# Four conditioning matmuls held together, and up-projection blocks of 384 columns with a copied halo

## The chip, the cores and the metric

The kernel runs on one core of one Trainium2 chip. The metric is device microseconds of one execution, and a kernel's time is the median of several runs. TensorE (PE) does the matmuls, VectorE (DVE) and ScalarE (ACT) read the results out of PSUM, GpSimd (POOL) works on SBUF alone, and SyncE (SP) issues the DMAs.

## The reference

A two-layer trunk runs one step for a prompt of 1024 positions and for 8 samples of 16 positions. The kernel treats the 1024 + 128 = 1152 rows together. Width is 1024, the MLP is 2816 wide, everything is fp32. What matters here is the conditioning and the channel mixer:

```
ada = sc @ w_ada[l] + b_ada[l]                  # sc = silu(c); one row for the prompt, eight for the samples
h = x * (1 + sc_f) + sh_f
u = h @ w_up                                    # 1024 -> 2 * 2816
y = conv_b
for tap in range(3):                            # causal depthwise convolution over positions
    y = y + conv_w[tap] * ue[:, tap : tap + T]  # ue = u with two rows of state in front
a, g = split(y)
out = (gelu(g) * a) @ w_down
x = layer_norm(ALPHA * x + (1 + gate) * out)
```

Position t of the convolution needs u at t, t-1 and t-2. So a block of positions needs the last two columns of the block ahead of it; these are called the halo here.

## The kernel before

The order of the work is: conditioning group 0; the first projection input; attention of layer 0 (sliding window); its output projection; the MLP of layer 0; attention of layer 1 (which begins with the key and value projections); its output projection; the MLP of layer 1.

**Split operands.** A product in nearly full fp32 is made from three products of rounded operands: each operand is split into a rounded high part and the rest (`split`, L147 to L151: ACT or DVE rounds, L149/L151; DVE or POOL subtracts, L160). `wload` brings one weight block of 512 KB into the ring `ws` of two slots and splits it into `wh` and `wl`. `mmT` (L265) multiplies one weight block with all of `H`: eight matmuls with `wl`, then sixteen with `wh`, 24 in all, into one PSUM bank, with positions as columns.

**Blocks of positions.** `BLK` cuts the 1152 positions in three blocks of 384. The key, query and other transposed projections use `BLK`. The up-projection uses its own cut, so that a block holds its halo by computing it again:

```
UB = ((0, 384), (380, 388), (764, 388))
```

**The MLP** (`ffn`). `up(j, gg)` loads one weight block of 128 up-projected channels, and calls `up_block` for the three blocks. There are 22 values of j and two halves gg (0 is `a`, 1 is the gated half), so 44 groups of channels in each layer. The three blocks take the PSUM banks 0, 1 and 2 in turn (`ub`). `conv` reads the bank: ACT takes the third tap and the bias (L980), DVE adds the other taps (L983; four shorter ones in the last block, which holds 256 prompt positions and the samples), and in the gated half ACT applies gelu (L1027), POOL multiplies (L1029), and ACT and DVE split the product for the down-projection (L149, L160). `down` (L1054, `dmm`) multiplies two groups into the row sums `acc` through the banks 3 to 5. The last pair of groups is done by `down_last`, in which the blocks of both halves alternate: block 0 of half 0, block 0 of half 1, block 1 of half 0, and so on, through the same three banks.

**Conditioning** (`ada`). Each of 7 groups of 2048 columns is made in 8 steps k. A step loads two weight blocks of 512 KB (L207), and issues four matmuls (L209), each with 32 stationary columns in its own quarter of the array (`tile_position=(0, 32 * j)`) and its own quarter of PSUM's partitions. Each of the four is two instructions in the trace, so a step is eight. Matmuls j = 0, 1 read the first block and j = 2, 3 the second. Group 0 runs at the start. Groups 1 and 2 are spread as background steps over attention 0, where their blocks use the two `ws` slots that the weights of the query projection use too; groups 3 to 6 are spread over the MLP of layer 0, with a ring of three slots of their own.

**Order.** The framework places every engine's instructions by a simulated timeline: at each point it takes from the ready ones the earliest in program order. It adds all semaphores, and it orders any two accesses of one PSUM bank. `issue_after(x)` holds an instruction back until x has been placed. Engines run their own queue in order, SP's DMA issues among them.

Of the kernel before, what the change touches and what calls it, by code (L numbers as in the profile page):

```python
# [20 lines left out]
BLK = ((0, 384), (384, 384), (768, 384))  # L21
# [66 lines left out]
class Trunk:  # L88
# [100 lines left out]
    def ada(self, gi, bank, ring=None, row=None):  # L189
        nc = self.nc  # L190
        ring = ring or self.ws
        ps = self.bank(bank)

        def load_bias(row):
            bsrc = self.I["adab"][gi : gi + 1, :]
            for j in range(4):
                nc.sync.dma_start(
                    row[32 * j : 32 * j + 32, 512:1024],
                    bass.AP(bsrc.tensor, bsrc.offset + j * 512, [[0, 32], [1, 512]]),
                )  # L200

        if row is not None:
            load_bias(row)
        for k in range(8):
            w = [ring.next() for _ in range(2)]
            for hf in range(2):
                nc.sync.dma_start(w[hf], self.I["adaw"][gi, k, hf])  # L207
            for j in range(4):
                nc.tensor.matmul(  # L209
                    ps[32 * j : 32 * j + 32, :],  # L210
                    self.cT[:, k * 32 : k * 32 + 32],
                    w[j // 2][:, (j % 2) * 512 : (j % 2) * 512 + 512],
                    start=k == 0,
                    stop=k == 7,
                    tile_position=(0, 32 * j),
                )
            yield
        if row is None:
            row = ring.next()
            load_bias(row)  # L220
        nc.vector.tensor_add(row[:, 0:512], ps, row[:, 512:1024])
        yield
        gate = {1: (0, 0), 2: (1, 2), 5: (2, 0), 6: (3, 2)}.get(gi)
        if gate is not None:
            g, j0 = gate
            for j2 in range(2):
                r = slice(32 * (j0 + j2), 32 * (j0 + j2) + 32)
                nc.gpsimd.tensor_scalar_add(row[r, 512:1024], row[r, 0:512], 1.0)
                nc.sync.dma_start(
                    self.gd[g, :, j2 * 512 : j2 * 512 + 512],  # L230
                    row[32 * (j0 + j2) : 32 * (j0 + j2) + 9, 512:1024],
                )
        for i in range(4):
            nc.tensor.transpose(ps[:, i * 128 : i * 128 + 128], row[:, i * 128 : i * 128 + 128], self.ident)
        dst = self.adaT[:, gi * 144 : gi * 144 + 144].rearrange("p (j i r) -> p i j r", j=4, i=4)
        nc.vector.tensor_copy(dst, ps.rearrange("p (i j r) -> p i j r", i=4, j=4)[:, :, :, 0:9])
        yield
# [710 lines left out]
    def ffn(self, l, xsrc, xdst, affs):  # L948
        nc, I, O, H = self.nc, self.I, self.O, self.H
# [26 lines left out]

        def conv(ps, cc, bi, y):
            w = lambda i: cw[:, cc, i : i + 1]
            off = 0 if bi == 0 else 4
            nc.scalar.activation(y, ps[:, off : off + 384], AF.Identity, bias=w(3), scale=w(2))  # L980

            def tap(o, u, i):
                nc.vector.scalar_tensor_tensor(o, u, w(i), o, op0=ALU.mult, op1=ALU.add)  # L983

            if bi == 0:
                tap(y[:, 1:384], ps[:, 0:383], 1)
                tap(y[:, 2:384], ps[:, 0:382], 0)
            elif bi == 1:
                tap(y, ps[:, 3:387], 1)
                tap(y, ps[:, 2:386], 0)  # L990
            else:
                tap(y[:, 0:256], ps[:, 3:259], 1)
                tap(y[:, 0:256], ps[:, 2:258], 0)
                ys = y[:, 256:384].rearrange("p (s q) -> p s q", q=16)
                us = ps[:, 260:388].rearrange("p (s q) -> p s q", q=16)
                tap(ys[:, :, 1:16], us[:, :, 0:15], 1)
                tap(ys[:, :, 2:16], us[:, :, 0:14], 0)
                nc.gpsimd.tensor_add(ys[:, :, 0:2], ys[:, :, 0:2], E4[:, cc])

        UB = ((0, 384), (380, 388), (764, 388))  # L1000

        acts = {}
        ya = {}
# [1 line left out]
        def up(j, gg):  # L1005
            w = self.wload(I["wup"][l, j + 22 * gg])
            for bi in range(3):
                up_block(w, j, gg, bi)

        def up_block(w, j, gg, bi):  # L1010
            cc = j + 22 * gg
            s0, n = UB[bi]
            ps = self.bank(ub.next())
            self.mmT(w, ps, s0, n)
            if gg == 0:
                y = ya[bi] = self.ya.next()
            else:
                y = self.yg.next()
            conv(ps, cc, bi, y)
            if bi == 2:  # L1020
                uo = self.uo[gg].rearrange("p (j s r) -> p j s r", s=9, r=2)
                src = ps[:, 258:402].rearrange("p (s q) -> p s q", q=16)[:, :, 0:2]
                nc.scalar.copy(uo[:, j % 11], src)
                if j % 11 == 10:
                    nc.sync.dma_start(O["conv"][l, gg, j // 11], self.uo[gg])
            if gg == 1:
                nc.scalar.activation(y, y, AF.Gelu_apprx_tanh)  # L1027
                a = self.at.next()
                nc.gpsimd.tensor_mul(a, y, ya[bi])  # L1029
                h, lo = aring.next()  # L1030
                self.split(a, h, lo, "a", "v")
                acts[(j, bi)] = (h, lo)
# [25 lines left out]
        def down_last():  # L1058
# [12 lines left out]
            for t in LO[l]:  # L1071
                for bi in UP[l].get(t, ()):
                    for gg in range(2):
                        up_block(wu[gg], NFF - 1, gg, bi)
                    if bi == 2:
                        w = [self.wring.next() for _ in range(2)]
                        for s, x in zip(wr, w):
                            self.split(s, *x, "a", "v")
# [267 lines left out]
```

## Time and profile before

| | |
|---|---|
| three runs | 3056.77, 3062.35 and 3062.54 us, median 3062.35 |
| profiled execution | 3055.63 us, of which the span of the instructions is 3053.6 us |
| PE busy | 2857.6 us, 94% of the span |
| DVE, ACT, POOL busy | 50%, 37%, 27% |
| mean granted TensorE clock | 0.968 |

The stages by the trace: conditioning group 0 and the first input up to about 100 us, attention 0 to 380, its output projection to 560, the MLP of layer 0 to about 1480, the key and value projections to 1650, attention 1 to 2020, its output projection to 2200, and the MLP of layer 1 to the end. In the timeline rows a line stands for a run of like instructions: start, length, engine, line, shape and count. The length goes to the modelled end of the last one, so the distance between matmuls is read from one row's start to the next row's start.

### The profile page before, as it was taken

Reading aid. Unit: us, or ns where it says so; the run is one execution under the profiler, and the core shown is the slowest. Engines: PE = TensorE matmul, PEld = TensorE weight load, DVE = VectorE, ACT = ScalarE, POOL = GpSimd, SP = SyncE. Lnnn points to the kernel's source line nnn. Section 1 sums busy time; section 2 is a strip of 40 time slices with the busy share of each in tenths; the row PEclk is TensorE's granted clock in tenths of the full one; section 3 lists DMA queues with packets and bytes.
Section 4 is the critical chain, followed back from the end, with each engine's and each line's share of the span. In section 5 each row is a group of like instructions: output and inputs, shape, how many; then the busy total and the mean of one; then the engine's idle time right before and its main releaser. Section 6 shows DMA issues by size and latency. Waiting matters only on the chain.

```text
span 3053.6 us, 42727 instructions
## 1 busy us (share of the span) xinstructions
PE 2857.6 (94%) x16524; PEld 2556.2 (84%) x16524; DVE 1516.3 (50%) x3162; ACT 1129.9 (37%) x2400; POOL 834.8 (27%) x599
## 2 busy tenths in 40 slices
PE   7999868899999999998999999966999999999996
PEld 4987656789888898997999988754899999999995
DVE  4355657524443443358412667655824444444468
ACT  2465613432222222224435766631432222222224
POOL 2011113422222222354651100102522222222253
PEclk8999888999999999999999999988999999999998
DMA  8555484622222222223785467778311111111121
GB/s 296 171 169 182 135 167 124 230 101 76 90 80 81 85 77 97 80 70 113 272 281 182 127 171 211 200 170 170 126 50 42 42 42 43 43 42 42 42 89 73
DMA packets 228235, 372.79 MB, mean 122 GB/s; under 512 B 35368, under 2 KB 149864, under 8 KB 227648
## 3 DMA queue, kind: packets, MB, share of 16 engines
q1 hardware_dynamic: 228032, 370.06, 39.6%
q8 instruction: 130, 2.13, 0.3%
q14 instruction: 73, 0.60, 0.1%
HBM read 294.65 MB, written 84.79 MB: 124 GB/s over the span
## 4 chain that ended last, share of the span: by engine, by line
PE 75%; DMA 9%; DVE 8%; SPq 3%; issue 2%; POOL 2%; ACT 2%; DVEq 0%; ACTq 0%; POOLq 0%
PE PS L265 45%; PE PS L1054 15%; PE PS L277 3%; PE PS L549 3%; PE PS L530 2%; PE PS L209 2%; PE PS L504 1%; DMA F<-rD 1%; SPq L923 1%; PE PS L507 1%; PE PS L651 1%; DMA x1att<-rD 1%; SPq L928 1%; POOL wl L160 1%; DVE F L944 1%
## 5 line engine op out<-in xcount | busy, mean ns | idle before, releaser
L265 PE MATMUL PS<-H,wh 128*128 128x384 f32 (+1 forms) x5472 | 1048.5, 339 | 0.3 <-DVE H L160 0.3
L265 PEld LDWEIGHTS PS<-H,wh 128*128 128x128 f32 x5472 | 968.1, 189 | 18.0 <-issue 9.2
L983 DVE SCALAR_TENSOR_TENSOR F<-PS,F 128x256 f32<-128x256 f32 (+2 forms) x704 | 353.1, 512 | 540.2 <-ACT F L980 527.1
L160 POOL TENSOR_TENSOR wl<-ws,wh 128x1024 fp32r<-128x1024 f32 x167 | 406.2, 2438 | 769.8 <-ACT wh L149 737.0
L265 PE MATMUL PS<-H,wl 128*128 128x384 f32 (+1 forms) x2736 | 570.2, 345 | 18.0 <-DVE H L151 7.9
L265 PEld LDWEIGHTS PS<-H,wl 128*128 128x128 f32 x2736 | 491.3, 191 | 49.7 <-issue 15.1
L1054 PE MATMUL PS<-wh,X 128*128 128x512 f32 x1584 | 465.5, 393 | 12.0 <-DVE acc L1045 4.2
L980 ACT ACTIVATE F<-PS,F 128x384 f32<-128x384 f32 x264 | 177.3, 672 | 744.4 <-PE PS L265 738.9
L1054 PEld LDWEIGHTS PS<-wh,X 128*128 128x128 f32 x1584 | 294.2, 188 | 73.1 <-issue 6.7
L1045 DVE TENSOR_TENSOR acc<-acc,PS 128x512 f32<-128x512 f32 x324 | 221.4, 686 | 268.8 <-PE PS L1054 268.2
L1029 POOL TENSOR_TENSOR F<-F 128x384 f32<-128x384 f32 x132 | 137.8, 1044 | 656.3 <-ACT F L1027 653.8
L1054 PE MATMUL PS<-wl,X 128*128 128x512 f32 x792 | 246.6, 392 | 0.0
L149 ACT CAST wh<-ws 128x1024 fp32r<-128x1024 f32 x176 | 182.2, 1045 | 139.0 <-PE PS L1054 75.1
L277 PE MATMUL PS<-wh,H 128*128 128x256 f32 (+1 forms) x1008 | 197.1, 325 | 36.9 <-DVE H L160 36.2
L277 PEld LDWEIGHTS PS<-wh,H 128*128 128x128 f32 x1008 | 153.3, 197 | 52.0 <-DVE H L160 37.4
L1054 PEld LDWEIGHTS PS<-wl,X 128*128 128x128 f32 x792 | 149.3, 188 | 33.2
L160 DVE TENSOR_TENSOR X<-F,X 128x384 fp32r<-128x384 f32 x132 | 111.2, 842 | 102.2 <-ACT X L149 101.9
L160 POOL TENSOR_TENSOR H<-F,H 128x1024 fp32r<-128x1024 f32 x23 | 60.3, 2622 | 257.6 <-ACT H L149 172.3
L470 DVE CUSTOM_DVE_ANT_0 F<-PS,F,C 128x256 f32<-128x256 f32 (+3 forms) x208 | 96.9, 480 | 60.8 <-PE PS L507 36.5
L530 PE MATMUL PS<-C,F 128*128 128x128 f32 x720 | 119.7, 281 | 5.5 <-DVE X L536 2.8
L1027 ACT ACTIVATE F<-F 128x384 f32<-128x384 f32 x132 | 69.1, 524 | 140.6 <-DVE F L983 128.2
L277 PE MATMUL PS<-x1att,H 128*128 128x512 f32 x432 | 114.5, 413 | 0.0
(196 smaller groups left out, 3119.3 us busy)
## 6 DMA issues: line engine op xcount, KB each, us to landing
ws<-in_wup_dram SPq DMA_DIRECT2D x88, 512.0 KB
F<-in_adaw_dram SPq DMA_DIRECT2D x74, 512.0 KB
ws<-in_wdn_dram SPq DMA_DIRECT2D x44, 512.0 KB
ws<-in_adaw_dram SPq DMA_DIRECT2D x32, 512.0 KB
X<-oT SPq DMA_DIRECT2D x64, 256.0 KB
x1att<-kH SPq DMA_DIRECT2D x60, 256.0 KB
xd<-F SPq DMA_DIRECT2D x27, 512.0 KB
F<-xd SPq DMA_DIRECT2D x27, 512.0 KB
```

The source lines that it names most:

```text
L149: nc.scalar.copy(out, in_)
L160: self.eng(el).tensor_sub(lo, src, hi.bitcast(F32))
L265: self.nc.tensor.matmul(out[:, 0:n], w[a][:, k * 128 : k * 128 + 128], H[:, p, k, s0 : s0 + n], start=i == 0, stop=i == 23)
L277: self.nc.tensor.matmul(out[:, 0:n], H[:, p, j * kn + k, t0 : t0 + 128], w[a][:, k * n : k * n + n], start=i == 0, stop=i == 23,)
L470: nc.vector.tensor_tensor_reduce(out=p[:, c0 : c0 + w], in0=ps, in1=b, scale=1.0, scalar=init, op0=ALU.add, op1=ALU.min, accum_out=nm)
L530: nc.tensor.transpose(t[:, m * 128 : m * 128 + 128], p[:, (kt - k0) * 128 : (kt - k0) * 128 + 128], self.ident)
L549: nc.tensor.matmul(ob[:, i0 * 128 : i0 * 128 + w], vst[a][:, kt, :], pp[:, m1 : m1 + w], start=cnt == 0, stop=cnt == 2 * len(order) - 1, s ...
L980: nc.scalar.activation(y, ps[:, off : off + 384], AF.Identity, bias=w(3), scale=w(2))
L983: nc.vector.scalar_tensor_tensor(o, u, w(i), o, op0=ALU.mult, op1=ALU.add)
L1029: nc.gpsimd.tensor_mul(a, y, ya[bi])
L1045: nc.vector.tensor_add(row[:, n], row[:, n], ps)
L1054: nc.tensor.matmul(ps, ac[m][p][:, cs], w[m][q][:, n], start=i == 0, stop=i == 5)
```

## The change

Two things change. In `ada` the four matmuls of a step are issued in the order j = 2, 3, 0, 1, and the last three are held behind the first, which reads the block that is loaded second. In `ffn` the up-projection uses the three blocks of 384 without overlap. In blocks 1 and 2 the matmuls write from column 2 of the bank, and ACT then copies the last two columns of the block before, from that block's PSUM bank, into columns 0 and 1. The columns that `conv` reads move by two.

```diff
-            for j in range(4):
-                nc.tensor.matmul(
...
+            lead = None
+            for j in (2, 3, 0, 1):
+                with ExitStack() as es:
+                    if lead is not None:
+                        es.enter_context(self.tc.issue_after(lead))
+                    mm = nc.tensor.matmul(
...
+                if lead is None:
+                    lead = mm.ins
...
-            off = 0 if bi == 0 else 4
+            off = 0 if bi == 0 else 2
...
-                tap(y, ps[:, 3:387], 1)
-                tap(y, ps[:, 2:386], 0)
+                tap(y, ps[:, 1:385], 1)
+                tap(y, ps[:, 0:384], 0)
...
-        UB = ((0, 384), (380, 388), (764, 388))
+        halo = {}
...
-            s0, n = UB[bi]
+            s0, n = BLK[bi]
             ps = self.bank(ub.next())
-            self.mmT(w, ps, s0, n)
+            off = 0 if bi == 0 else 2
+            self.mmT(w, ps[:, off:512], s0, n)
+            if bi:
+                nc.scalar.copy(ps[:, 0:2], halo.pop(cc))
+            if bi < 2:
+                halo[cc] = ps[:, off + 382 : off + 384]
...
-                src = ps[:, 258:402].rearrange("p (s q) -> p s q", q=16)[:, :, 0:2]
+                src = ps[:, 256:400].rearrange("p (s q) -> p s q", q=16)[:, :, 0:2]
```

More of the change, by code (lines that the diff above doesn't have):

```diff
@@ L207, in ada @@
                 nc.sync.dma_start(w[hf], self.I["adaw"][gi, k, hf])
-            for j in range(4):
[L209 to L216, printed above, removed]
+            lead = None
[4 more added lines that the diff above has]
+                    mm = nc.tensor.matmul(
+                        ps[32 * j : 32 * j + 32, :],
+                        self.cT[:, k * 32 : k * 32 + 32],
+                        w[j // 2][:, (j % 2) * 512 : (j % 2) * 512 + 512],
+                        start=k == 0,
+                        stop=k == 7,
+                        tile_position=(0, 32 * j),
+                    )
+                if lead is None:
+                    lead = mm.ins
             yield
@@ L988, in conv @@
             elif bi == 1:
-                tap(y, ps[:, 3:387], 1)
-                tap(y, ps[:, 2:386], 0)
-            else:
-                tap(y[:, 0:256], ps[:, 3:259], 1)
-                tap(y[:, 0:256], ps[:, 2:258], 0)
+                tap(y, ps[:, 1:385], 1)
+                tap(y, ps[:, 0:384], 0)
+            else:
+                tap(y[:, 0:256], ps[:, 1:257], 1)
+                tap(y[:, 0:256], ps[:, 0:256], 0)
                 ys = y[:, 256:384].rearrange("p (s q) -> p s q", q=16)
-                us = ps[:, 260:388].rearrange("p (s q) -> p s q", q=16)
+                us = ps[:, 258:386].rearrange("p (s q) -> p s q", q=16)
                 tap(ys[:, :, 1:16], us[:, :, 0:15], 1)
```

## The prediction

> **What bounds the kernel now.** I read the page first, for the engine on which the end hangs, and then the busy time by stage, since the change touches stages that may have different limits. The page's busy times and its chain of waits by line:
>
> ```profile
> span 3053.6 us, 42727 instructions
> PE 2857.6 (94%) x16524; PEld 2556.2 (84%) x16524; DVE 1516.3 (50%) x3162; ACT 1129.9 (37%) x2400; POOL 834.8 (27%) x599
> ...
> PE PS L265 45%; PE PS L1054 15%; PE PS L277 3%; PE PS L549 3%; PE PS L530 2%; PE PS L209 2%; PE PS L504 1%; DMA F<-rD 1%; SPq L923 1%; PE PS L507 1%; PE PS L651 1%; DMA x1att<-rD 1%; SPq L928 1%; POOL wl L160 1%; DVE F L944 1%
> ```
>
> PE is busy for 94% of the span, and the chain that ended last runs mostly through it: 45% in the transposed projections (L265, the up-projection among them), 15% in the down-projection (L1054), and 2% in the conditioning matmuls (L209). The stretches of attention 0 and of the steady part of both MLPs (PE, PEld, DVE, ACT, POOL busy with counts, then granted clock, DMA share, GB/s):
>
> ```profile
> 100.00:380.00 280.00, 266.85 (x1992) 218.39 (x1991) 156.30 (x525) 170.14 (x514) 35.10 (x46) 0.97 0.50 159
> ...
> 560.00:1390.00 830.00, 827.88 (x4354) 738.48 (x4353) 341.80 (x573) 226.24 (x379) 246.28 (x186) 1.00 0.28 95
> ...
> 2200.00:2940.00 740.00, 739.62 (x3907) 698.73 (x3906) 312.74 (x542) 220.19 (x372) 216.17 (x165) 1.00 0.14 46
> ```
>
> In the MLPs PE has work for 827.88 of 830 us and 739.62 of 740 us, at full clock. There a shorter PE stream shortens the run one for one. Attention 0 has 13 us without PE work in 280, so PE is nearly the bound there too, but less firmly.
>
> **Up-projection blocks.** The matmuls of a steady stretch of the second MLP, block by block (8 with `wl`, 16 with `wh`):
>
> ```profile
> 2370.08 1.57 PE L265 MATMUL PS<-H,wl 128*128 128x384 f32 x8
> 2371.49 2.93 PE L265 MATMUL PS<-H,wh 128*128 128x384 f32 x16
> 2374.26 1.58 PE L265 MATMUL PS<-H,wl 128*128 128x388 f32 x8
> 2375.68 2.99 PE L265 MATMUL PS<-H,wh 128*128 128x388 f32 x16
> 2378.51 1.57 PE L265 MATMUL PS<-H,wl 128*128 128x388 f32 x8
> ...
> 2382.75 1.58 PE L265 MATMUL PS<-H,wl 128*128 128x384 f32 x8
> ```
>
> From start to start, sixteen matmuls of 384 columns take 2374.26 - 2371.49 = 2.77 us, 173.1 ns each; sixteen of 388 take 2378.51 - 2375.68 = 2.83 us, 176.9 ns each. Four columns cost 3.8 ns where their share of a 384-column matmul would be 173.1 x 4/384 = 1.8 ns. A channel group of three blocks takes 2382.75 - 2370.08 = 12.67 us. Its first eight matmuls, of 384 columns behind a 388 block, also run at 1.41/8 = 176 ns. The key projection runs the same helper on 384, 384, 384:
>
> ```profile
> 1502.16 1.55 PE L265 MATMUL PS<-H,wl 128*128 128x384 f32 x8
> ...
> 1514.64 1.55 PE L265 MATMUL PS<-H,wl 128*128 128x384 f32 x8
> ```
>
> Three such blocks take 1514.64 - 1502.16 = 12.48 us. So a group of the new blocks should take 12.48 us, 0.19 us less. There are 44 x 2 = 88 groups, whose 388-column matmuls are these:
>
> ```profile
> L265 PE MATMUL PS<-H,wh 128*128 128x388 f32 x2816 | 535.5, 339 | 0.0
> ...
> L265 PE MATMUL PS<-H,wl 128*128 128x388 f32 x1408 | 290.4, 340 | 0.0
> ```
>
> (2816 + 1408)/48 = 88. The upper end is 88 x 0.19 = 16.7 us. The lower end with a benefit counts the columns alone: 4224 x 1.8 ns = 7.6 us. The difference is whether the extra 2 ns come with the ragged source (column 380 and length 388, which go) or with something that stays. One thing here is in no row: the output starts two columns into its bank. If that costs what the ragged 388 costs over 384, the gain is gone; that is the other end, 0. I see no reason for it to cost, and the nearest row is the 384-only stream, so I take 15 us.
>
> By the Trainium skill ("TensorE: Matmul & The Clock Gate", "Back-to-back issue gap") the isolated gap between warm matmuls is N/2.4 + 2.5 ns, so four columns would be worth 1.7 ns and this term 4224 x 1.7 = 7.0 us, an estimate from that page. The trace does not agree: its 173.1 to 176.9 ns is twice that.
>
> **The halo copy.** 176 ACT copies of 2 columns are added. The nearest row is the smallest copy from PSUM:
>
> ```profile
> L1023 ACT COPY F<-PS 128x18 f32<-128x18 f32 x88 | 15.3, 174 | 95.5 <-DVE F L983 95.5
> ```
>
> At 174 ns that is 31 us of ACT, hidden where ACT has slack: in 2200 to 2940 it is busy 220 of 740 us. The copy stands on ACT's queue ahead of the block's own L980, so conv starts 0.17 us later; nothing on PE waits for it, because a bank comes round after three blocks. Bank k is now also held until block k+1 has finished and the copy has run, 4.2 us longer than its matmuls, and it is wanted again 8.4 us after. The copy must also follow DVE's taps on bank k; PE's first matmuls of two later blocks, and the taps:
>
> ```profile
> 2391.18 1.58 PE L265 MATMUL PS<-H,wl 128*128 128x388 f32 x8
> ...
> 2395.42 1.58 PE L265 MATMUL PS<-H,wl 128*128 128x384 f32 x8
> ```
>
> ```profile
> 2392.09 1.27 DVE L983 SCALAR_TENSOR_TENSOR F<-PS,F 128x384 f32<-128x384 f32 x2
> ```
>
> These taps belong to the block that ended at 2391.18 and are through at 2393.36, 2 us before the next block ends at 2395.42. I take 0 in the steady part; without that cover it would be 0.17 us a block, 30 us in all.
>
> The cover is missing in one place. In `down_last` the halves alternate through the same three banks, so the fourth block (block 1 of half 1) takes bank 0, which the copy behind the third block reads; and the last block takes bank 2 from which the copy behind the fifth reads. PE's rows for these two starts, then ACT's:
>
> ```profile
> 2993.61 1.57 PE L265 MATMUL PS<-H,wl 128*128 128x388 f32 x8
> ...
> 3009.63 1.58 PE L265 MATMUL PS<-H,wl 128*128 128x388 f32 x8
> ```
>
> ```profile
> 2994.80 0.51 ACT L149 CAST X<-F 128x384 fp32r<-128x384 f32 x1 [1.42 <-POOL F L1029]
> 2995.22 0.67 ACT L980 ACTIVATE F<-PS,F 128x384 f32<-128x384 f32 x1
> ...
> 3009.83 0.67 ACT L980 ACTIVATE F<-PS,F 128x384 f32<-128x384 f32 x1 [1.06 <-PE PS L265]
> ```
>
> Today PE goes on at 2993.61 and 3009.63 without idling. After the change the fourth block waits until ACT has made a copy for the third. ACT had a cast waiting for POOL in its queue until 2994.80 and reached the third block's L980 at 2995.22. With the copy at that place the bank is free at 2995.4, a stall of 1.8 us; if the copy is put ahead of the cast, 0.2 us of latency (as at 3009.83) and 0.17 us. The second place costs about 0.4 us. That is 0.8 to 2.2 us for a layer; behind the stall are the remaining blocks of the last pair and the normalisations. I take 4 us for both layers.
>
> **Conditioning.** A step's matmuls run together where they are adjacent. The first MLP has both cases, a pair of matmuls (four instructions) and all four (eight):
>
> ```profile
> 592.94 1.05 PE L209 MATMUL PS<-F,C 128*32 128x512 f32 x4
> 593.92 2.91 PE L265 MATMUL PS<-H,wh 128*128 128x388 f32 x15
> ...
> 663.09 1.07 PE L209 MATMUL PS<-F,C 128*32 128x512 f32 x8
> 664.08 1.68 PE L265 MATMUL PS<-H,wl 128*128 128x384 f32 x8
> ```
>
> The pair holds PE for 593.92 - 592.94 = 0.98 us; the four hold it for 0.99 us. So a step cut in two costs one more burst of 0.98 us. How many are cut follows from the busy time of L209 in both stretches:
>
> ```profile
> 100.00:300.00 200.00, 28.46 (x128) 4.06 (x128) 1.00 0.52 166
> 560.00:1390.00 830.00, 42.82 (x256) 6.48 (x256) 1.00 0.28 95
> ```
>
> A burst shows 1.05 us busy, so 42.82 us in the MLP are about 41 bursts for 32 steps (256/8), and 28.46 us in attention 0 are about 27 for 16. All four in one burst would save 9 x 0.98 = 8.8 us and 11 x 0.98 = 10.8 us. In the MLP nothing else on PE is waiting to come between, and its three slots are its own: I take 8, with 0 as the other end. In attention it is less sure. One step there:
>
> ```profile
> 118.05 1.05 PE L209 MATMUL PS<-ws,C 128*32 128x512 f32 x4
> 119.03 0.39 PE L504 MATMUL PS<-x1att 128*128 128x256 f32 x1
> ...
> 124.91 1.04 PE L209 MATMUL PS<-ws,C 128*32 128x512 f32 x2
> 125.88 0.33 PE L530 MATMUL PS<-C,F 128*128 128x128 f32 x1
> ...
> 126.69 1.04 PE L209 MATMUL PS<-ws,C 128*32 128x512 f32 x2
> ```
>
> It is cut into a pair and two singles, between which transposes came. `issue_after` only keeps three behind the first; it doesn't keep others out. I take half, 5 us.
>
> At the start the hold costs nothing, because each pair waited for its own block, and the last:
>
> ```profile
> 27.51 1.05 PE L209 MATMUL PS<-x1in,C 128*32 128x512 f32 x4 [0.23 <-DMA x1in<-in_adaw_dram]
> ```
>
> Its pair starts when the second block lands, as the four will then.
>
> **Sum**, against the profiled execution: 15 + 8 + 5 - 4 = 24 us off 3055.63 gives 3031.6 us. The median of the runs shown, 3062.35, lies 6.7 us above that execution (the lowest, 3056.77, 1.1 us above), so the forecast for a median is 3038 us.
>
> **Rivals.** *The offset output keeps the cost.* For it: no row has such an output, and the first eight matmuls of a group are dear although they have 384 columns. Against: the 384-only stream. With the 7.6 us end the sum is 16.6, 3046 us; at the 0 end 3053 us. Chance 0.15.
>
> *The hold doesn't hold.* The order of j changes, but others still come between, as often as now. Then only 15 - 4 = 11 remain, 3051 us. Attention's singles speak for it, the MLP's many whole steps against it. Chance 0.10.
>
> *Slower: the weights of the query projection come late.* In attention the conditioning blocks share two slots with those weights, and SP's queue is in order. The next load takes the slot of the step's first block, and in the step shown above SP issued it just after the first pair:
>
> ```profile
> 119.14 0.33 SPq L164 DMA_DIRECT2D ws<-in_wq_dram  x1
> ```
>
> It was then split by ACT and POOL, and PE used it:
>
> ```profile
> 123.73 2.37 POOL L160 TENSOR_TENSOR wl<-ws,wh 128x1024 fp32r<-128x1024 f32 x1 [24.25 <-ACT wh L149]
> ```
>
> ```profile
> 130.29 1.55 PE L265 MATMUL PS<-H,wl 128*128 128x384 f32 x8
> ```
>
> Held together, the slot comes free only behind the last matmul, 126.69 + 0.98 = 127.7, which is 8.5 us later; POOL would end at 126.1 + 8.5 = 134.6, and PE, ready at 130.29, would be 4.3 us short. Behind this load on SP's queue are the bias loads and the next conditioning loads. Seven such loads make 30 us at worst, and attention's 5 us are lost: 3062.35 - 19 + 30 = 3073 us. It decides from 19/7 = 2.7 us a load. Against it: a query block is needed only about eight pieces of work later, and the placement by simulated timeline fills PE with other work meanwhile. Chance 0.10.
>
> *No change*: these together in part, the offset at its worst and a few stalls. Chance 0.07.
>
> **How the numbers follow.** The forecast, with its terms between their ends, has the remaining 0.58. Gains of 16.7 + 8.8 + 10.8 less 1.6 of stalls are 34.7 us; from the lowest run that reaches 3022 us. The upper end takes in the two rivals that are faster and the case of no change, to 3057 us, and leaves out the slower one. 0.2% is 6.1 us, about what a measurement of this kernel can tell from no change: faster by more is 0.58 + 0.15 + 0.10 = 0.83, the same 0.07, slower 0.10.
>
> **What the profile after would show.** A channel group in the second MLP's steady part takes 12.48 us from first to first matmul if the main term is right; 12.57 or more means that the offset costs. L209 is busy about 33 us in the first MLP's stretch, and its rows there all count eight. In attention 0, fewer and larger L209 rows; PE idle time there that ends with a weight split (POOL wl) would show the slower rival. In `down_last`, PE has a gap ahead of the fourth and the sixth block, ended by the ACT copy; a gap like that in the steady part would prove the cover wrong. The prediction is wrong if PE's busy share of the MLP stretches falls, or if attention 0 gets longer.

## The result, and the profile after

The change makes the kernel slower: 3074.33 us median of 6 runs (3073.58 to 3083.36), against 3055.99 us for the kernel before (6 runs, 3052.64 to 3062.54). The ratio is 1.0063, with a 95% interval of 1.0045 to 1.0080. The forecast was 3038 us, set off from the three runs' median of 3062.35 us, with a range that ended at 3057. The profiled execution after took 3074.2 us, 18.6 us more than the one before. The page after:

```profile
span 3072.4 us, 42957 instructions
...
PE 2840.4 (92%) x16524; PEld 2542.1 (83%) x16524; DVE 1535.6 (50%) x3162; ACT 1146.2 (37%) x2576; POOL 830.2 (27%) x599
...
PE PS L271 37%; PE PS L1065 15%; PE PS L283 2%; PE PS L555 2%; PE PS L536 2%; SPq L929 1%; PE PS L213 1%; DMA F<-in_xrow_dram 1%; PE PS L510 1%; DVE F L950 1%; DMA X<-oT 1%; PE PS L513 1%; DMA F<-rD 1%; DVE C L815 1%; DVE acc L1125 1%
```

PE does less work than before (2840.4 us busy, 2857.6 before) and ends later: its share went from 94% to 92%. So the work was shortened and more than the saving came back as waits. The same three stretches as in the prediction (PE, PEld, DVE, ACT, POOL busy with counts, granted clock, DMA share, GB/s):

```profile
100.00:380.00 280.00, 268.56 (x2004) 218.73 (x2003) 151.16 (x522) 166.50 (x511) 35.13 (x48) 0.99 0.47 149
...
560.00:1390.00 830.00, 817.61 (x4359) 733.56 (x4360) 359.60 (x586) 234.31 (x465) 255.15 (x189) 0.99 0.28 97
...
2200.00:2940.00 740.00, 733.66 (x3899) 690.75 (x3898) 327.27 (x538) 230.65 (x458) 221.66 (x166) 1.00 0.15 50
```

In both MLPs PE is no longer without gaps: 817.61 of 830 us and 733.66 of 740 us. Where the 18.8 us of span came from is seen by following the same PE events through the timelines of both (us from the start of the span, the start of a first matmul and the end of a last one; the last four columns are the difference to before for kernels that are told of below):

| event | before | after | difference | hold only | blocks only | early halo, old last pair | hold in attention 0 only |
|---|---|---|---|---|---|---|---|
| last values matmul of attention 0 | 373.3 | 382.0 | +8.7 | +7.4 | -2.3 | +0.3 | +7.6 |
| first up-projection matmul, layer 0 | 540.5 | 546.2 | +5.6 | +3.9 | +0.6 | +0.3 | +5.8 |
| last down-projection matmul, layer 0 | 1456.3 | 1460.7 | +4.4 | -0.7 | +0.9 | -9.0 | +4.4 |
| first up-projection matmul, layer 1 | 2191.4 | 2198.6 | +7.2 | 0.0 | +2.5 | -8.0 | +10.4 |
| last down-projection matmul, layer 1 | 3034.4 | 3058.1 | +23.7 | +2.0 | +17.6 | -9.0 | +13.1 |
| end | 3053.6 | 3072.4 | +18.8 | +0.6 | +13.5 | -10.0 | +12.2 |

There are two losses: 8.7 us in attention 0, and 16.5 us from the first up-projection to the last down-projection of layer 1. The first MLP is only 1.2 us shorter, although the conditioning should have given it 8 us on its own. Of the 16.5 us, 6.6 lie ahead of the second down-projection group, 4.4 are gained from there to the first matmul of the last group, and 14.3 lie from there to the last down-projection matmul. The table compares single executions: two pairs of kernels told of in experiment 6, whose matmuls stand in the same order, differ by up to 5.9 us at these points and by up to 4.2 us in the length of one stage.

**The matmuls did what was forecast.** PE's rows in a steady stretch of the second MLP after the change:

```profile
2383.96 1.55 PE L271 MATMUL PS<-H,wl 128*128 128x384 f32 x8
2385.34 2.93 PE L271 MATMUL PS<-H,wh 128*128 128x384 f32 x16
2388.11 1.55 PE L271 MATMUL PS<-H,wl 128*128 128x384 f32 x8
...
2392.28 1.55 PE L271 MATMUL PS<-H,wl 128*128 128x384 f32 x8
...
2396.44 1.55 PE L271 MATMUL PS<-H,wl 128*128 128x384 f32 x8
```

Sixteen matmuls take 2388.11 - 2385.34 = 2.77 us, the first eight of a group 1.38 us (1.41 before), and a group of three blocks 2396.44 - 2383.96 = 12.48 us. That is the key projection's value to the digit. The group's three blocks take 4.15, 4.17 and 4.16 us, and the last two write from column 2 on, so an output that begins two columns into its bank costs nothing. But the whole period (four groups of up-projection, 108 down-projection matmuls) is shortened by less than 4 x 0.19 = 0.76 us. The chains of before, then after, from the first down-projection of one period to that of the next:

```profile
2408.26 4.11 PE PS L1054 x18
...
2483.69 4.11 PE PS L1054 x18
```

```profile
2421.56 4.12 PE PS L1065 x18
...
2496.52 4.12 PE PS L1065 x18
```

The period was 75.43 us and is 74.96 us, 0.47 us less. Counted over six periods of each trace, the up-projection's matmuls gave back 0.71 us a period and the down-projection's cost 0.24 us more. PE changes from down- to up-projection 15 times a period, 8 times before: the placement cut the down-projection in smaller pieces. The last 512-column matmul ahead of such a change takes 234.6 ns to the next start in the mean, where it was 226.7 ns; that the smaller pieces are what costs is not shown.

**The halo copy is cheap.** Its group on the page (busy, mean ns, idle before):

```profile
L1023 ACT COPY PS<-PS 128x2 f32<-128x2 f32 x176 | 25.6, 145 | 415.2 <-PE PS L271 392.2
```

It takes 145 ns where 174 was assumed; the 176 of them are 25.6 us of ACT. What costs is how long they keep a bank, as experiment 3 shows.

**The start of an MLP.** Before, while the last rows of `H` were still being made, PE ran ahead to the next channel groups. PE's rows at the start of the second MLP, before:

```profile
2201.29 1.65 PE L265 MATMUL PS<-H,wl 128*128 128x384 f32 x8 [0.38 <-POOL F L966]
...
2206.34 1.66 PE L265 MATMUL PS<-H,wl 128*128 128x388 f32 x8
...
2210.67 1.58 PE L265 MATMUL PS<-H,wl 128*128 128x384 f32 x8
...
2214.16 1.58 PE L265 MATMUL PS<-H,wl 128*128 128x388 f32 x8
```

A 384-column run is block 0 of a group, so these are block 0 and block 1 of the second group, and block 0 of the third. The last row is block 2 of the first group: ACT's cast of the last rows of `H` starts at 2211.95, and DVE's taps of 256 columns, which only block 2 has, follow the run at 2219.32. PE leaves out block 2 until its rows are there, and hardly waits. After:

```profile
2203.72 1.55 PE L271 MATMUL PS<-H,wl 128*128 128x384 f32 x8
2205.10 2.94 PE L271 MATMUL PS<-H,wh 128*128 128x384 f32 x16
2210.27 1.62 PE L271 MATMUL PS<-H,wl 128*128 128x384 f32 x8 [2.23 <-ACT PS L1023]
...
2219.42 2.50 PE L271 MATMUL PS<-H,wl 128*128 128x384 f32 x8 [3.87 <-ACT H L149]
2221.71 3.71 PE L271 MATMUL PS<-H,wh 128*128 128x384 f32 x16
2225.66 1.66 PE L271 MATMUL PS<-H,wl 128*128 128x384 f32 x8 [0.23 <-ACT PS L1023]
```

ACT's rows there:

```profile
2209.98 0.14 ACT L1023 COPY PS<-PS 128x2 f32<-128x2 f32 x1
...
2218.28 1.08 ACT L149 CAST H<-F 128x1024 fp32r<-128x1024 f32 x1
...
2225.46 0.14 ACT L1023 COPY PS<-PS 128x2 f32<-128x2 f32 x1 [2.15 <-PE PS L271]
```

The run at 2203.72 is block 1 of the first group. The next one is block 0 of the second group, in bank 0, and it waits 2.23 us for the copy at 2209.98, which reads the first group's columns out of bank 0. The copy in turn had to wait for DVE's taps on that bank, which end at 2209.89, so little of this wait is its own. Then PE waits 3.87 us for the last rows of `H` (ACT's cast at 2218.28) before it can do block 2 of the first group: block 1 of the second group cannot be taken ahead of it, since bank 1 is held for the first group's block 2. That next run starts at 2225.66, behind the copy at 2225.46. The prediction had a bank "wanted again 8.4 us after", which holds only while PE goes through the blocks in order.

**The end of an MLP.** PE's rows in the last pair of layer 1, then ACT's:

```profile
2997.42 1.55 PE L271 MATMUL PS<-H,wl 128*128 128x384 f32 x8
2998.81 2.94 PE L271 MATMUL PS<-H,wh 128*128 128x384 f32 x16
3005.03 2.93 PE L271 MATMUL PS<-H,wl 128*128 128x384 f32 x8 [3.28 <-ACT PS L1023]
...
3010.85 0.39 PE L1065 MATMUL PS<-wh,X 128*128 128x512 f32 x1
...
3014.29 1.57 PE L271 MATMUL PS<-H,wl 128*128 128x384 f32 x8
...
3021.04 1.75 PE L271 MATMUL PS<-H,wh 128*128 128x384 f32 x9
3022.62 0.63 PE L1065 MATMUL PS<-wh,X 128*128 128x512 f32 x2
...
3026.74 1.57 PE L271 MATMUL PS<-H,wl 128*128 128x384 f32 x8
...
3048.13 0.80 PE L1065 MATMUL PS<-wh,X 128*128 128x512 f32 x1 [9.04 <-DVE X L160]
```

```profile
3004.82 0.15 ACT L1023 COPY PS<-PS 128x2 f32<-128x2 f32 x1
...
3022.82 0.14 ACT L1023 COPY PS<-PS 128x2 f32<-128x2 f32 x1 [0.55 <-PE PS L271]
...
3045.14 0.49 ACT L149 CAST X<-F 128x384 fp32r<-128x384 f32 x1
```

The fourth block, at 3005.03, waits 3.28 us for the copy at 3004.82, which stood on ACT's queue behind casts that wait for POOL. The prediction had found this place and put 1.8 us on it. It had not found that the fifth block's bank is held too, by the copy behind the fourth: that block began right behind the fourth before, and now begins 3.4 us after it, at 3014.29, with down-projection matmuls between from 3010.85 on. Nor had it found what happens to the sixth block: down-projection matmuls stand between it and the fifth (whose last piece is at 3021.04), and it begins at 3026.74 in place of immediately. Its product is split by ACT only at 3045.14, between the normalisations, and the last down-projection matmuls wait 9.04 us for it. In the early-save kernel of experiment 3, with the same last pair, the fifth and the sixth block begin right behind the block ahead (2993.85 and 3005.62), and PE's longest wait in the down-projection behind them is 1.68 us: it is the held bank that moves them. That it does so because the placement's simulated timeline does not have the bank free is inferred from the order. From the last down-projection group's first matmul to the end of the span it is 82.6 us, 73.2 us before.

**The conditioning.** Busy time of its matmuls in the MLP of layer 0 and in attention 0:

```profile
560.00:1390.00 830.00, 36.18 (x256) 5.31 (x256) 0.99 0.28 97
100.00:380.00 280.00, 28.30 (x128) 4.00 (x128) 0.99 0.47 149
```

In the MLP 42.82 us became 36.18, 6.6 us less, and these matmuls stand in 34 rows, 30 of them of eight, where there were 38. In attention 0 the rows fell from 31 to 26, but the busy time only from 28.46 to 28.30 us.

### The profile page after: what moved, and what is told of

It reads as the page before. It is cut to its first block, busy times and chain, and to the rows that moved or that the text cites. A ratio compares the mean times of both kernels' runs of the same rounds, so it can differ in the third digit from the quotient of the medians.

```text
span 3072.4 us, 42957 instructions
## 1 busy us (share of the span) xinstructions
PE 2840.4 (92%) x16524; PEld 2542.1 (83%) x16524; DVE 1535.6 (50%) x3162; ACT 1146.2 (37%) x2576; POOL 830.2 (27%) x599
## 4 chain that ended last, share of the span: by engine, by line
PE 62%; DVE 9%; DMA 7%; ACT 3%; SPq 2%; issue 2%; POOL 2%; DVEq 0%; ACTq 0%; POOLq 0%
PE PS L271 37%; PE PS L1065 15%; PE PS L283 2%; PE PS L555 2%; PE PS L536 2%; SPq L929 1%; PE PS L213 1%; DMA F<-in_xrow_dram 1%; PE PS L510 1%; DVE F L950 1%; DMA X<-oT 1%; PE PS L513 1%; DMA F<-rD 1%; DVE C L815 1%; DVE acc L1125 1%
## 5 line engine op out<-in xcount | busy, mean ns | idle before, releaser
L271 PE MATMUL PS<-H,wh 128*128 128x384 f32 x5472 | 1049.7, 337 | 0.3 <-DVE H L160 0.3
L271 PE MATMUL PS<-H,wl 128*128 128x384 f32 x2736 | 560.8, 342 | 44.8 <-DVE H L151 10.6
L1065 PE MATMUL PS<-wh,X 128*128 128x512 f32 x1584 | 480.2, 397 | 18.0 <-DVE X L160 10.1
L160 DVE TENSOR_TENSOR X<-F,X 128x384 fp32r<-128x384 f32 x132 | 138.6, 1050 | 113.3 <-ACT X L149 112.9
L1023 ACT COPY PS<-PS 128x2 f32<-128x2 f32 x176 | 25.6, 145 | 415.2 <-PE PS L271 392.2
```

What stands on the lines that cost most here:

```text
L160: self.eng(el).tensor_sub(lo, src, hi.bitcast(F32))
L271: self.nc.tensor.matmul(out[:, 0:n], w[a][:, k * 128 : k * 128 + 128], H[:, p, k, s0 : s0 + n], start=i == 0, stop=i == 23)
L1065: nc.tensor.matmul(ps, ac[m][p][:, cs], w[m][q][:, n], start=i == 0, stop=i == 5)
```

## Experiments

Theory A, after this reading: each half of the change brings a loss of its own, the blocks at the starts and ends of the MLPs because of the held banks, the hold in attention 0. Theory B: the hold brings almost the whole loss, and the blocks are a gain. Ratios are to the kernel before on the same chip. Each has 10 runs, blocks only 4.

| kernel | median us | ratio | 95% interval |
|---|---|---|---|
| hold only | 3054.36 | 1.0005 | 0.9995 to 1.0016 |
| blocks only | 3068.88 | 1.0055 | 1.0038 to 1.0073 |
| hold in the MLP of layer 0 only | 3046.77 | 0.9981 | 0.9970 to 0.9992 |
| blocks, halo saved early | 3051.52 | 0.9998 | 0.9984 to 1.0012 |
| blocks, halo saved early, old last pair | 3044.35 | 0.9961 | 0.9947 to 0.9976 |
| blocks, halo from the held bank, old last pair | 3058.03 | 1.0006 | 0.9992 to 1.0019 |
| early halo, old last pair, hold in the MLP | 3045.86 | 0.9963 | 0.9950 to 0.9976 |
| hold in attention 0 only | 3063.65 | 1.0025 | 1.0012 to 1.0038 |
| hold in attention 0 only, natural order | 3053.93 | 0.9996 | 0.9986 to 1.0005 |
| order alone in attention 0, no hold | 3064.65 | 1.0026 | 1.0015 to 1.0037 |
| hold at the start only | 3057.34 | 1.0004 | 0.9991 to 1.0016 |

**1. The two halves apart.** The first has the new loop in `ada` and the old `UB`; the second the old loop and the new blocks.

> The hold of the four conditioning matmuls alone, with the old overlapping blocks. Theory A (each half of the change brings its own loss: the hold in attention 0, the blocks at the ends of the MLPs): attention 0 ends about 9 us later as in the changed kernel, the MLP of layer 0 gets about 6.6 us of L209 time back (36.2 instead of 42.8 us busy), so +2 us in all, 3058 us against 3056. Theory B (the hold brings nearly the whole loss, the blocks are a gain): +25 us or more, 3080 us.

> The 384-column blocks with the copied halo alone, conditioning as before. Theory A: the steady groups gain about 0.115 us each (10 us over 88), but starts and ends of both MLPs lose more, +12 to +17 us in all, about 3070 us. Theory B: only the steady gain is left, -10 us, 3046 us.

The hold alone is 1.0005, the blocks alone 1.0055. Theory B falls: the blocks are no gain, they bring nearly the whole loss. The hold alone loses 7.4 us in attention 0 and has it back by the end of the first MLP, 4.6 us of it within that MLP.

**2. The hold where PE is never idle.** Only the conditioning groups that run in the first MLP are held:

```diff
+            for j in (2, 3, 0, 1) if gi > 2 else range(4):
...
+                    if lead is not None and gi > 2:
```

> The hold for the conditioning groups 3 to 6 alone, which run in the MLP of layer 0; groups 0 to 2 (the start and attention 0) as before, old blocks. Theory A: start and attention 0 as before, the MLP's L209 rows all of eight, -6 to -8 us, 3049 us. Rival: a placement that changes anywhere moves the stages behind it by several us either way, so the gain is swallowed and the time is 3056 us or more.

0.9981: some 5 us are gained, a little less than was expected. The conditioning's busy time in the first MLP is 38.25 us, 4.6 less, in 36 rows; 28 of them, not all, are of eight. Attention 0 is as before (-1.1 us).

**3. Held banks or something else in the blocks.** ACT saves the two columns into a small SBUF tile straight behind the block's own matmuls, and copies them from there:

```diff
             if bi < 2:
-                halo[cc] = ps[:, off + 382 : off + 384]
+                halo[cc] = self.halo.next()
+                nc.scalar.copy(halo[cc], ps[:, off + 382 : off + 384])
```

> Blocks as in the blocks-only kernel, but ACT saves the last two columns of each block into SBUF straight behind that block's own matmuls, and copies them from there into the next block's bank; 176 more ACT copies of 145 ns, and no bank is held past its own conv. If the held banks cause the loss at the ends of the MLPs (PE waiting for L1023), the last up block of layer 1 ends as early as in the kernel before and the run is some 10 us faster than blocks only, about 3050 us. If the loss is the later conv alone or a reshuffled order, it stays within 3 us of blocks only.

The ratio falls from 1.0055 to 0.9998, some 17 us, with twice the copies. So the cost is in how long a bank is kept, not in the copies and not in the ragged or offset columns. But it is only level with before.

**4. The last pair.** In the last pair of channel groups the blocks are the old overlapping ones, without a halo copy; elsewhere the halo is saved early (first kernel) or taken from the held bank (second):

```diff
+            last = j == NFF - 1
+            s0, n = (UB if last else BLK)[bi]
...
+            if bi and not last:
+                nc.scalar.copy(ps[:, 0:2], halo.pop(cc))
```

> Blocks of 384 with the halo saved early into SBUF, but the last channel pair (down_last) with the old overlapping blocks. If the halo's steps in the last pair are what lengthens the end of each MLP (from the tenth down-projection on 79.7 us in the early-halo kernel, 73.2 in the kernel before), the ends go back to 73 us and the run is 6 to 12 us under the kernel before, 3042 us. If the end gets longer for another reason (a reshuffled order), it stays at 3051 us.

> Blocks of 384 with the halo copied out of the held PSUM bank as in the change, but the last channel pair with the old overlapping blocks; conditioning as before. If the held banks hurt only in the last pair, this is as fast as the early halo with the old last pair, 3042 us. If they also hurt at the start of each MLP, where PE could run ahead to the next channel group while the last rows of H are still being made, the start of the MLP of layer 1 (first up-projection matmul to the second down-projection) stays 5 us longer than before, in both MLPs, and this is 8 to 10 us slower than the early one, 3051 us.

With experiments 1 and 3 this is a square of four kernels: held bank or early save, new or old last pair. The old last pair gains 0.0049 with the held bank (1.0055 to 1.0006) and 0.0037 with the early save (0.9998 to 0.9961), 15 and 11 us. The early save gains 0.0057 with the new last pair and 0.0045 with the old one, 17 and 14 us. Each of these four differences is uncertain by about 0.002, 6 us. So both places count, and within that they add. PE's rows at the start of the second MLP in the kernel with both cures:

```profile
2194.82 1.85 PE L267 MATMUL PS<-H,wl 128*128 128x384 f32 x8 [2.05 <-POOL F L968]
...
2201.44 1.63 PE L267 MATMUL PS<-H,wl 128*128 128x384 f32 x8
...
2205.69 1.55 PE L267 MATMUL PS<-H,wl 128*128 128x384 f32 x8
```

After one wait of 2.05 us PE runs ahead again as it did before the change. The row puts this wait down to POOL, but DVE's taps on bank 0, which the run writes, also end just ahead of it, at 2194.67; it stands where the changed kernel waited 2.23 us. The table of events has this kernel 9 us ahead of before by the end of the first MLP. With the old last pair the held bank was expected to cost 8 to 10 us. The ratios say 14 us, the two profiled executions 8.2 us (spans of 3051.8 and 3043.6 us). In these two, the starts, from the first up-projection to the second down-projection group, account for 2.9 us in the first and 3.8 us in the second MLP. Another 5.5 us lies between the second and the last group of the first MLP, where the conditioning stands in 39 rows in place of 37; it was not followed further. Why the halo still costs 11 us in the last pair when no bank is held is not settled: the end of the second MLP explains 3.8 us of it in the traces, and the rest lies ahead of it, in the first MLP and the seams around it.

**5. Do the gains add?** The kernel with both cures, and the hold in the first MLP:

> The early halo with the old last pair, and the hold for the conditioning groups 3 to 6 alone. If the gains add up: 5 us from the hold and 6 to 12 us from the blocks, 3036 us. If a reshuffled order eats one of them, 3046 us.

0.9963 against 0.9961 without the hold: no further gain is seen, within intervals of 0.0013 each way. Its profiled execution is 3.7 us the shorter, so a gain of that size is neither shown nor excluded. Both are 0.4% faster than the kernel before, and by the ratios 1.0% faster than the changed one.

**6. Why attention 0 gets longer.** First the hold in attention 0 alone (groups 1 and 2), then the same with the matmuls in the order 0, 1, 2, 3, then the order 2, 3, 0, 1 without a hold:

```diff
-            for j in (2, 3, 0, 1) if gi in (1, 2) else range(4):
+            for j in range(4):
```

> The hold for the conditioning groups 1 and 2 alone, which run in attention 0; all else as before. If the hold in attention 0 brings the delay there (shared weight slots freed later, loads late), the last values matmul of attention 0 comes 5 to 8 us later than in the kernel before and the run is 3057 us. If the delay comes from the start (group 0 held, PE's clock lower until 70 us), attention 0 is unchanged within 1 us and the run 3051 us.

> The hold in attention 0 alone (groups 1 and 2), but with the matmuls in the order 0, 1, 2, 3, so that the first one needs only the block that is loaded first. If attention 0 gets longer because all four wait for the second block and give the shared weight slot back late, it is as before here: last values matmul within 2 us of the kernel before, run 3056 us. If any change of the placement there costs, it comes 5 to 8 us later, run 3063 us.

> No hold at all, but in attention 0 (groups 1 and 2) the four matmuls in the order 2, 3, 0, 1. The slot of the first block is then given back last. If the late slot is the cause, attention 0 ends 5 to 8 us later as with the hold, 3063 us; if it is the hold's constraint, it ends within 2 us of before, 3056 us.

The order alone costs 1.0026 and ends attention 0 11.6 us later; the hold in natural order costs nothing (0.9996, 3.0 us earlier). It is the order, not the hold. The traces say more: with the hold in natural order PE's matmuls stand in the same order, line by line, as in the kernel before, and with the order 2, 3, 0, 1 they stand in the same order with the hold and without it. So in attention 0 the hold does nothing, and the 3.0 us and the 4.0 us between the two later ends are differences between executions. The framework orders any two accesses of one PSUM bank, and the four matmuls write one bank, which may be why. Whether the order alone also gathers the steps in the first MLP was not tried. With j = 2 first, the slot of the first block, which the next weight load takes, is given back last. SP's issues of the fifth and the sixth load for the query projection, before and then with the hold in attention 0 alone:

```profile
233.55 0.37 SPq L164 DMA_DIRECT2D ws<-in_wq_dram  x1
...
257.90 0.33 SPq L164 DMA_DIRECT2D ws<-in_wq_dram  x1
```

```profile
250.10 0.33 SPq L164 DMA_DIRECT2D ws<-in_wq_dram  x1
...
269.71 0.33 SPq L164 DMA_DIRECT2D ws<-in_wq_dram  x1
```

They come 16.6 and 11.8 us later. With the order alone they come 19.8 and 15.2 us later, with the hold in natural order 0.7 us earlier. The placement fills PE with other work meanwhile, but cannot fill all of it. That the late slot is the link between the order and the delay fits these issues and is not shown by itself; a kernel with slots of their own for the conditioning was not tried.

**7. The start.** Only group 0 is held:

> The hold for conditioning group 0 alone, at the start. If four matmuls together leave PE idle long enough for its clock to be lowered, the later bursts of the start take 1.93 us in place of 1.06 us as in the changed kernel, and the first scores of attention 0 come 2 to 3 us later; at most 3 us of it reach the end, 3058 us against 3055. If the start is bound by its loads alone, as the prediction has it, the first scores come within 0.5 us of before.

By the lengths of the bursts the clock is low for most of the start, but nothing reaches the end (1.0004; first scores 0.2 us earlier). PE's rows and the stretch from 20 to 30 us, granted clock third from the end:

```profile
22.37 1.07 PE L213 MATMUL PS<-x1in,C 128*32 128x512 f32 x8 [0.85 <-DMA x1in<-in_adaw_dram]
24.94 1.94 PE L213 MATMUL PS<-x1in,C 128*32 128x512 f32 x8 [1.50 <-DMA x1in<-in_adaw_dram]
27.49 1.94 PE L213 MATMUL PS<-x1in,C 128*32 128x512 f32 x8 [0.61 <-DMA x1in<-in_adaw_dram]
```

```profile
20.00:30.00 10.00, 6.46 (x32) 0.58 (x27) 0.51 (x1) 1.04 (x1) 0.00 (x0) 0.73 1.04 421
```

The four together take 1.93 or 1.94 us in the first four bursts, from 8.45 on, 1.07 us only at 22.37, and 1.94 us again from 24.94 on. So the 3.2 us by which the scores began later after the change do not come from the hold at the start alone; they were not followed further.

## Why the prediction was wrong

**Up-projection columns: right in the matmul, too large in the sum.** The step from 388 to 384 columns gives 12.48 us a group, as taken from the key projection, and the offset output is free. The term, 15 us, was mis-sized: a period of four groups gains 0.47 us, so 88 groups give 10 us. The prediction took PE's order in the mixed stretch as fixed; it changed, and the down-projection's matmuls there take 0.24 us a period more.

**The halo copy: this is the step that failed.** "I take 0 in the steady part" is right for the second MLP, where a period with held banks and one with the early save are equal to 0.01 us. "The cover is missing in one place" is not: there is a second, the start of each MLP, where PE's order was bound by rows of `H` and not by banks, and where the held bank takes away the room to run ahead. The square of experiment 4 puts 14 to 17 us on the held banks; the traces place 5 to 7 us of it at the two starts. In the one place that was named, the sum had 4 us for both layers and the measured cost with the held bank is 15 us: the wait ahead of the fourth block was 3.28 us instead of 1.8, and the fifth and the sixth block, whose banks are held as well, lost their places in the order, so that normalisations came ahead of the sixth one's split. The prediction looked for a stall ahead of the sixth block; what came there was another order.

**Conditioning in the MLP: right, a little large.** 6.6 us less busy time in the changed kernel; alone 4.6 us less and a ratio of 0.9981, some 5 us, against 8 us.

**Conditioning in attention 0: wrong sign.** The 5 us did not come (0.16 us of busy time did), and 7 to 9 us were lost there, up to 12 with the order alone. The rival "the weights of the query projection come late" named the shared slots and SP's queue, and got 0.10; its price of 30 us was the worst case without other work for PE, and a quarter of it was paid. It blamed the hold, which does nothing there. The order of j is what brings the loss, and the order was in the diff. That this rival's 3073 us is nearly the measured time is chance: attention 0 gave 8.7 us of the loss, and most of the rest came from the blocks.

**The start: right that it costs nothing at the end,** though its reason was incomplete, since the bursts themselves got longer.

**Rivals.** The slower side was given only to attention. That a bank which is read later is a bank that comes free later was worked out for steady blocks and the last pair, and not as a rival; it decided the result. Both of the prediction's own signs of being wrong came: PE's busy share of the MLP stretches fell, and attention 0 got longer.

## What to carry to other kernels

A tiny read can be expensive by when it happens: ask of every buffer who holds it until when, and look not only at the steady part but at the first and last rounds, where the order is bound by other things and the free buffers are what lets an engine run ahead. Save such a scrap early into a place of its own. And when parts of a step are reordered so that they can start together, look at which input slot is then given back last, and at the queue behind it.

## What the runs showed of the hardware

In experiment 7 the clock was lowered although PE was never idle for long. Around the one fast burst, at 22.37, PE is busy for 1.07 us of the 2.57 us to the next start, 42%; it is idle for 0.85 us ahead of it and 1.50 us behind it, and the granted clock from 20 to 30 us is 0.73. With the pairs, 1.05 us in every 1.28, it is 1.00 there. The Trainium skill ("TensorE: Matmul & The Clock Gate", "What's actually happening") has the clock lowered after at least one idle window of about 3.4 us. If that is read as one unbroken gap, the trace does not agree: from the second burst on no idle time in front of one is above 1.73 us.

PSUM output that starts 8 bytes into a bank costs nothing: in the group shown above each 384-column matmul takes 173 ns from start to start, in the blocks with the offset as in the one without. And 388 columns from a start that is not on the block's edge take 3.8 ns more than 384 (176.9 against 173.1 ns, from rows rounded to 0.01 us), where their share of the columns would be 1.8 ns.
